# Taking the two column halves in turn: scan, banded heads, sparse heads and delta rule

## The chip, the cores and the metric

The kernel runs on one core of one Trainium2 chip, as one program. The metric is the device time of one execution in microseconds (us): the median over the runs shown. The trace is that of one further execution, taken with the hardware profiler. In what follows TensorE (rows of matmuls: PE, of weight loads: PEld) multiplies matrices into PSUM banks, VectorE (DVE), ScalarE (ACT) and GpSimd (POOL) work on tiles, and SyncE (SP) issues transfers.

## The reference, cut to what matters

Four layers on 512 tokens of width 1024, at batch 1. The first block is one layer with an SSD scan and differential attention, and one with retention and sliding-window attention; the second block has two layers, each with a gated delta rule, native sparse attention and stick-breaking attention, and a feed-forward part. Everything is float32. The changed products belong to these lines, head by head (all heads concerned are 64 wide; of the delta rule the kernel forms the products of `w` with the decayed keys and with the attention ahead of its recurrence):

```python
# scan: 16 heads in 4 groups, chunks of 128
y_diag = jnp.einsum("bclsg,bclsgr,bcsgrp->bclgrp", cb, decay_in, X)      # within a chunk
y_off = jnp.einsum("bclgn,bcgrpn,bclgr->bclgrp", Cc, state_prev, jnp.exp(a_cs))
# banded heads: 8 query heads, 2 key groups, window 128
out = jnp.einsum("bngrqk,bnkgd->bnqgrd", p, vb)
# delta rule: 6 heads, chunks of 64, state (64, 64)
v_new = u_i - jnp.einsum('bhcd,bhde->bhce', w_i, state)
# sparse heads: 6 query heads, 2 key groups, a selected and a window branch
o_s = jnp.einsum('bgrqn,bgqnd->bqgrd', p_s.astype(v_sel.dtype), v_sel)
o_w = jnp.einsum('bgrqn,bngd->bqgrd', p_w.astype(vw.dtype), vw)
```

## The kernel before

Activations lie feature-major: 128 features on the partitions, 512 tokens along the columns, one tile per 128 features. A projection (`fm`, lines 432 to 444) takes one unit of weights, splits it into a high and a low part (lines 409 and 411) and makes 24 products of 128x512 (`mm3`, lines 415 to 420: three for each of 8 chunks). These are the products of most of TensorE's time. Work of the heads stands between them.

Two heads of 64 features share one tile of 128 partitions. Where a product writes only one head, its stationary operand has 64 columns and its result goes to partitions 0 to 63 or 64 to 127 of a PSUM bank: to one half of the array's columns. Such a product of float32 operands is two instructions in the trace, each with its own weight load. A transpose is one. The four places that the change touches:

- **Scan** (`ssd`, line 848; products at 951 and 953). For each of 4 groups and 2 pairs of heads (`j`), a head `hh` makes `seg` (lines 938 to 943: one product into bank `s`, four VectorE subtractions, an exponential, a product with `cb`) and `ea` (lines 944 to 946), then for each of 4 chunks one product with `xdt` and, but for the first, one with the state `st`, all into its half of `py` (bank `o`). `seg` has two buffers, `ea` one.
- **Banded heads** (`swa`, line 1117; products at 1162). For each of 4 rounds `r` and 2 key groups `g`: the bias tile `stt` is loaded, then 4 query blocks go one after another through scores (lines 518, 519, bank `s`), VectorE's evacuation with the maximum (1150), ScalarE's exponential (1151), a scale (1155), one or two transposes (1158, bank `d`), a copy (1160) and the products. The tile `sl` has three buffers.
- **Delta rule** (`gdn_pair`, line 1331; products at 1469 and 1470). Of a pair of heads, head by head, 4 chunk pairs of two products each, into the banks `pA` and `pq` (bank `d`, two buffers). VectorE makes `aTz` of `pA` (1477), on which the recurrence over chunks rests.
- **Sparse heads** (`nsa_heads`, line 1639; products at 1671). For each of 3 heads `r`, 2 branches and 2 key groups: 4 query blocks with 1 to 4 key blocks each. The steps are those of the banded heads: scores, evacuation into `nl` (1660, 128 to 512 columns), exponential (1661), clamp, reciprocal and scale (1662 to 1664), transposes (1667, bank `t`, one buffer), copy into `npt` (1669), products into `po`, which accumulates over both branches. The `nl` tile's ring `nx` has three buffers.

Not changed, but of the same kind: the stick-breaking heads' products at line 1767 (loop from 1764) go over 4 key blocks and, inside, over the two heads, with 512, 384, 256 and 128 columns.

What sets the order: the program is written out once, and the tile framework arranges each engine's instructions ahead of time, by the place in the program and by when operands and buffers come free; products into one PSUM tile keep the program's order, and work on other tiles can be put between. On the chip each engine works its list in order. The list `ORDER` (line 305) says in which turn the delta rule (`g0` to `g2`), the inputs (`i`) and the sparse heads (`n0` to `n2`) are written, one stretch up to the next `yield` at a time. In `ssd` and `retention` the `fill` calls put an output projection's step between the heads' work.

Of the kernel before, what the change touches and what calls it, by code (L numbers as in the profile page):

```python
# [7 lines left out]
F32 = mybir.dt.float32  # L8
# [6 lines left out]
T = 512  # L15
# [326 lines left out]
class Build:  # L342
# [505 lines left out]
    def ssd(self, hs, p, outs, fill):  # L848
        nc = self.nc
# [29 lines left out]
        ps = self.bank("d")  # L879
# [8 lines left out]
        for g in range(4):  # L888
# [43 lines left out]
            nc.vector.tensor_mul(cb, ps, tri.rearrange("p (o l) -> p o l", o=1).to_broadcast([128, 4, 128]))  # L932
            for j in range(2):
                py = self.bank("o")
                for hh in range(2):
                    h = 4 * g + 2 * j + hh
                    pb = self.bank("s", [128, 4, 128])
                    nc.tensor.matmul(pb, sel[:, h:h + 1].to_broadcast([48, 128]), acsT, start=True, stop=True)
                    sg = p.tile([128, 4, 128], F32, tag="seg", name="seg", bufs=2)
                    for b in range(4):  # L940
                        nc.vector.tensor_scalar(sg[:, b], pb[:, b], acs[:, b, h:h + 1], 0.0, SUB, MIN)
                    nc.scalar.activation(sg, sg, ACTF.Exp)
                    nc.vector.tensor_mul(sg, sg, cb)
                    ea = p.tile([128, T], F32, tag="ea", name="ea")
                    nc.scalar.activation(ea, pb.rearrange("p b l -> p (b l)"), ACTF.Exp)
                    nc.vector.tensor_mul(ea, ea, ct)
                    c0 = 64 * (2 * j + hh)
                    for b in range(4):
                        s = slice(128 * b, 128 * b + 128)
                        o = py[64 * hh:64 * hh + 64, s]  # L950
                        nc.tensor.matmul(o, xdt[:, b, c0:c0 + 64], sg[:, b], start=True, stop=b == 0)
                        if b:
                            nc.tensor.matmul(o, st[:, b - 1, c0:c0 + 64], ea[:, s], start=False, stop=True)
                fill('ce'[j])
                y = outs.tile([128, T], F32, tag=f"s{2 * g + j}", name="ssdy")
                nc.vector.scalar_tensor_tensor(y, xts[j], self.V("eD")[:, 2 * g + j:2 * g + j + 1], py, MUL, ADD)
                for _, ps in self.fm("e_ssd", 6 * g + 4 + j, hs, side=True):
                    e = self.sigmoid(p, ps)
                    nc.vector.tensor_mul(e, e, ps)
                    nc.vector.tensor_mul(y, y, e)  # L960
                fill('df'[j])
                yield y
# [154 lines left out]
    def swa(self, hs, p, outs):  # L1117
# [15 lines left out]
        for r in range(4):  # L1133
            for _, ps in self.fm("o_sw", 2 + r, hs):
                qt = self.stack_left(p, "sqt", ps, 0.125, bufs=2)
            po = self.bank("o")
            for g in range(2):
                h = 4 * g + r
                gs = slice(64 * g, 64 * g + 64)
                tt = p.tile([128, 256], F32, tag="stt", name="stt", bufs=2)  # L1140
                nc.sync.dma_start(tt, self.t5[h][:, 256:512])
                nc.vector.tensor_add(tt, tt, self.C("wmask"))
                for i in range(4):
                    n = 256 if i else 128
                    k0 = 128 * (i - 1) if i else 0
                    s = self.bank("s")
                    self.scores(s[:, :256], qt, kt, g, slice(128 * i, 128 * i + 128), slice(k0, k0 + 256))
                    l = p.tile([128, 256], F32, tag="sl", name="sl", bufs=3)
                    sm = p.tile([128, 4], F32, tag="ssm", name="ssm", bufs=3)
                    nc.vector.tensor_tensor_reduce(l[:, :n], s[:, :n], tt[:, 256 - n:], -1.0, ns[:, h:h + 1], ADD, MIN, sm[:, 0:1])  # L1150
                    nc.scalar.activation(l[:, :n], l[:, :n], ACTF.Exp, bias=sm[:, 0:1], scale=-1.0, accum_out=sm[:, 1:2])
                    nc.scalar.activation(sm[:, 2:3], ns[:, h:h + 1], ACTF.Exp, bias=sm[:, 0:1], scale=-1.0)
                    nc.vector.tensor_add(sm[:, 3:4], sm[:, 1:2], sm[:, 2:3])
                    nc.vector.reciprocal(sm[:, 3:4], sm[:, 3:4])
                    nc.vector.tensor_scalar(l[:, :n], l[:, :n], sm[:, 3:4], None, MUL)
                    pt = self.bank("d", [128, 4, 128])
                    for j in range(n // 128):
                        nc.tensor.transpose(pt[:, j], l[:, 128 * j:128 * j + 128], ident)
                    ptt = p.tile([128, 2, 128], F32, tag="sptt", name="sptt", bufs=3)
                    nc.scalar.copy(ptt[:, :n // 128], pt[:, :n // 128])  # L1160
                    for j in range(n // 128):
                        nc.tensor.matmul(po[gs, 128 * i:128 * i + 128], vt[:, k0 // 128 + j, gs], ptt[:, j],
                                         start=j == 0, stop=j == n // 128 - 1)
            o = outs.tile([128, T], F32, tag="o", name="wo", bufs=5)
            nc.scalar.copy(o, po)
            yield o
# [164 lines left out]
    def gdn_pair(self, l, pr, hs, ab, p, outs, outs_):  # L1331
# [130 lines left out]
            nc.gpsimd.memset(qz[par][:, :, par2[1 - par]], 0.0)  # L1462

        pA, pq = pst(), pst()
        for hh in range(2):
            o = slice(64 * hh, 64 * hh + 64)
            for b in range(4):
                t = slice(128 * b, 128 * b + 128)
                mm(pA[o, t], wu[:, hh, b, 0:64], kdz[:, b, :, hh], start=True, stop=True)
                mm(pq[o, t], wu[:, hh, b, 0:64], attz[:, hh, b], start=True, stop=True)  # L1470


        aT = t8("nlt")
# [165 lines left out]
    def nsa_heads(self, l, r, st, p, on):  # L1639
# [7 lines left out]
        rr = slice(64 * (r % 2), 64 * (r % 2) + 64)  # L1647
        mm(po, st["vcb"][rr], st["ptc"][rr, r // 2], start=True, stop=False)
        for bi, br in enumerate("sw"):
            for g in range(2):  # L1650
                yield
                gs = slice(64 * g, 64 * g + 64)
                for i in range(4):
                    n = 128 * (i + 1)
                    s = self.bank("s")
                    w = max(n, 256)
                    self.scores(s[:, :w], ql, ks[br], g, slice(128 * i, 128 * i + 128), slice(0, w))
                    lt = p.tile([128, T], F32, tag="nx", name="nl", bufs=3)
                    sm = p.tile([128, 3], F32, tag="nsm", name="nsm", bufs=4)
# [2 lines left out]
                    nc.vector.tensor_scalar(sm[:, 1:2], sm[:, 1:2], 1e-30, None, MAX)  # L1662
                    nc.vector.reciprocal(sm[:, 2:3], sm[:, 1:2])
                    nc.vector.tensor_scalar(lt[:, :n], lt[:, :n], sm[:, 2:3], gates[:, i, 1 + bi, r, g:g + 1], MUL, MUL)
                    ps = self.bank("t", [128, 4, 128])
                    for j in range(i + 1):
                        nc.tensor.transpose(ps[:, j], lt[:, 128 * j:128 * j + 128], ident)  # L1667
                    pt = p.tile([128, 4, 128], F32, tag="npt", name="npt", bufs=2)
                    nc.scalar.copy(pt[:, 0:i + 1], ps[:, 0:i + 1])
                    for j in range(i + 1):  # L1670
                        mm(po[gs, 128 * i:128 * i + 128], vt[:, j, bi, gs], pt[:, j], start=False, stop=bi == 1 and i == 3 and j == 3)  # L1671
        yield
        o = qs
        nc.scalar.copy(o, po)
# [310 lines left out]
```

## Time and profile before

| | us |
|---|---|
| median of 3 runs | 3457.21 |
| lowest, highest run | 3454.8, 3462.34 |
| the profiled execution, its own time | 3465.89 |
| its span, first to last instruction | 3464.2 |
| TensorE matmul busy in the span | 3330.6 |
| VectorE busy | 2210.1 |
| ScalarE busy | 1693.8 |

Busy time is the union of an engine's instructions, so that overlapping ones count once. Matmuls are pipelined, and their ends are modelled: the duration of a matmul's row is longer than the step to the next matmul, and what a row of matmuls costs is read from their starts. A timeline row with xN merges N neighbours of one line: its length runs from the first one's start to the last one's end. Times in the timeline are us from the span's start.

### The profile page before, as it was taken

Reading aid. Unit: us, or ns where it says so; the run is one execution under the profiler, and the core shown is the slowest. Engines: PE = TensorE matmul, PEld = TensorE weight load, DVE = VectorE, ACT = ScalarE, POOL = GpSimd, SP = SyncE. Lnnn points to the kernel's source line nnn. Section 1 sums busy time; section 2 is a strip of 40 time slices with the busy share of each in tenths; the row PEclk is TensorE's granted clock in tenths of the full one; section 3 lists DMA queues with packets and bytes.
Section 4 is the critical chain, followed back from the end, with each engine's and each line's share of the span. In section 5 each row is a group of like instructions: output and inputs, shape, how many; then the busy total and the mean of one; then the engine's idle time right before and its main releaser. Section 6 shows DMA issues by size and latency. Waiting matters only on the chain. (4 is left out here: it accounts for less than half of the span.)

```text
span 3464.2 us, 45651 instructions
## 1 busy us (share of the span) xinstructions
PE 3330.6 (96%) x17752; PEld 2620.7 (76%) x17752; DVE 2210.1 (64%) x3650; ACT 1693.8 (49%) x2962; POOL 298.2 (9%) x204
## 2 busy tenths in 40 slices
PE   8999998999989998999899999999989999999997
PEld 4877775888868876888667777888877777788885
DVE  6678775544476655444566765776776676677676
ACT  4665554322365445222355557544455565654444
POOL 2000111000110002000201001000030100200002
PEclk9999998999999999999999999999999999999998
DMA  7343212532333442322221002232322100233322
GB/s 261 117 144 105 72 61 68 171 121 92 100 107 105 157 135 99 97 91 98 79 77 62 19 28 84 93 97 98 98 88 74 62 19 22 79 98 98 98 91 76
DMA packets 97112, 323.93 MB, mean 94 GB/s; under 512 B 10936, under 2 KB 12472, under 8 KB 96768
## 3 DMA queue, kind: packets, MB, share of 16 engines
q1 hardware_dynamic: 96160, 319.44, 28.5%
q8 instruction: 140, 2.29, 0.3%
q10 hardware_dynamic: 576, 1.05, 0.1%
q14 instruction: 76, 0.62, 0.1%
q0 software_dynamic: 160, 0.52, 0.0%
HBM read 313.61 MB, written 9.98 MB: 93 GB/s over the span
## 5 line engine op out<-in xcount | busy, mean ns | idle before, releaser
L409 ACT CAST whi<-wr 128x1024 fp32r<-128x1024 f32 x459 | 480.3, 1048 | 884.9 <-PE pss L419 421.8
L411 DVE TENSOR_TENSOR wlo<-wr,whi 128x1024 fp32r<-128x1024 f32 x409 | 501.9, 1228 | 388.8 <-ACT whi L409 384.6
L418 PE MATMUL psg<-hh,whi 128*128 128x512 f32 x1448 | 582.9, 403 | 8.1 <-DVE gu L837 7.4
L420 PE MATMUL psg<-hh,wlo 128*128 128x512 f32 x1448 | 577.7, 399 | 0.0
L419 PE MATMUL psg<-hl,whi 128*128 128x512 f32 x1448 | 576.7, 398 | 0.0
L418 PE MATMUL pss<-hh,whi 128*128 128x512 f32 x784 | 310.7, 399 | 31.1 <-ACT hh L475 11.3
L418 PEld LDWEIGHTS psg<-hh,whi 128*128 128x128 f32 x1448 | 274.3, 189 | 69.2 <-issue 8.8
L420 PEld LDWEIGHTS psg<-hh,wlo 128*128 128x128 f32 x1448 | 273.4, 189 | 58.8 <-issue 6.7
L419 PEld LDWEIGHTS psg<-hl,whi 128*128 128x128 f32 x1448 | 273.7, 189 | 57.4 <-issue 7.3
L419 PE MATMUL pss<-hl,whi 128*128 128x512 f32 x784 | 312.3, 398 | 3.3 <-DVE hl L482 3.3
L420 PE MATMUL pss<-hh,wlo 128*128 128x512 f32 x784 | 311.0, 397 | 0.0
L334 POOL TENSOR_TENSOR sqacc<-sqacc,sq 128x512 f32<-128x512 f32 x86 | 130.3, 1515 | 1703.4 <-ACT sq L332 1702.5
L418 PE MATMUL psg<-mh,whi 128*128 128x512 f32 x560 | 223.7, 400 | 1.1 <-DVE x L680 1.0
L420 PE MATMUL psg<-mh,wlo 128*128 128x512 f32 x560 | 220.7, 395 | 0.0
L419 PE MATMUL psg<-ml,whi 128*128 128x512 f32 x560 | 220.2, 394 | 0.0
L418 PEld LDWEIGHTS pss<-hh,whi 128*128 128x128 f32 x784 | 150.2, 192 | 70.2 <-ACT hh L475 16.0
L419 PEld LDWEIGHTS pss<-hl,whi 128*128 128x128 f32 x784 | 151.1, 193 | 38.5 <-DVE hl L482 4.9
L411 POOL TENSOR_TENSOR wlo<-wr,whi 128x1024 fp32r<-128x1024 f32 x50 | 122.8, 2456 | 631.4 <-ACT whi L409 631.4
L420 PEld LDWEIGHTS pss<-hh,wlo 128*128 128x128 f32 x784 | 150.7, 192 | 33.8 <-issue 2.0
L418 PE MATMUL pss<-mh,whi 128*128 128x512 f32 x432 | 170.9, 396 | 0.5 <-DVE x L680 0.5
L420 PE MATMUL pss<-mh,wlo 128*128 128x512 f32 x432 | 169.8, 393 | 0.0
L419 PE MATMUL pss<-ml,whi 128*128 128x512 f32 x432 | 169.7, 393 | 0.0
(628 smaller groups left out, 6399.7 us busy)
## 6 DMA issues: line engine op xcount, KB each, us to landing
wr<-w SPq DMA_DIRECT2D x128, 512.0 KB, 3.5
wr<-up SPq DMA_DIRECT2D x88, 512.0 KB, 3.4
mw<-modw SPq DMA_DIRECT2D x80, 512.0 KB, 3.8
wr<-in SPq DMA_DIRECT2D x48, 512.0 KB, 3.5
wr<-down SPq DMA_DIRECT2D x40, 512.0 KB, 3.5
wr<-e_ssd SPq DMA_DIRECT2D x24, 512.0 KB, 3.5
wr<-e_qk SPq DMA_DIRECT2D x16, 512.0 KB, 4.1
mw<-modw SPq DMA_DIRECT2D x32, 256.0 KB, 5.4
```

Of the source, the lines that this page charges most:

```text
L334: nc.gpsimd.tensor_add(self.acc, self.acc, sq)
L409: self.nc.scalar.copy(hi, raw)
L411: eng.tensor_sub(lo, raw, hi.bitcast(F32))
L418: mm(ps, ws[0], xs[0], start=first, stop=False)
L419: mm(ps, ws[0], xs[1], start=False, stop=False)
L420: mm(ps, ws[1], xs[0], start=False, stop=last)
```

## The change

In all four places two products that write different halves now follow each other. In the scan both heads' `seg` and `ea` are made first, then each chunk's products are issued for head 0 and head 1; the second head's `ea` takes a slot of the shared ring `pt` (three buffers). In the banded heads the loop over key groups moves inside the loop over query blocks; both bias tiles are loaded first (`stt` has four buffers instead of two), the transposes of both groups go to one bank, and one copy (`sptt`, two buffers of twice the size instead of three) serves both. In the delta rule the loops over chunk pairs and heads change places. In the sparse heads the loop over key groups moves inside too; transposes, copies and products go by up to two key blocks of both groups at a time, and the `yield`s move from before each group to before query blocks 0 and 3.

```diff
@@ -932,6 +932,7 @@
             nc.vector.tensor_mul(cb, ps, tri.rearrange("p (o l) -> p o l", o=1).to_broadcast([128, 4, 128]))
             for j in range(2):
                 py = self.bank("o")
+                sgs, eas = [], []
                 for hh in range(2):
                     h = 4 * g + 2 * j + hh
                     pb = self.bank("s", [128, 4, 128])
@@ -941,16 +942,21 @@
                         nc.vector.tensor_scalar(sg[:, b], pb[:, b], acs[:, b, h:h + 1], 0.0, SUB, MIN)
                     nc.scalar.activation(sg, sg, ACTF.Exp)
                     nc.vector.tensor_mul(sg, sg, cb)
-                    ea = p.tile([128, T], F32, tag="ea", name="ea")
+                    ea = self.nb.tile([128, T], F32, tag="pt", name="ea", bufs=3) if hh else p.tile([128, T], F32, tag="ea", name="ea")
                     nc.scalar.activation(ea, pb.rearrange("p b l -> p (b l)"), ACTF.Exp)
                     nc.vector.tensor_mul(ea, ea, ct)
-                    c0 = 64 * (2 * j + hh)
-                    for b in range(4):
-                        s = slice(128 * b, 128 * b + 128)
-                        o = py[64 * hh:64 * hh + 64, s]
-                        nc.tensor.matmul(o, xdt[:, b, c0:c0 + 64], sg[:, b], start=True, stop=b == 0)
-                        if b:
-                            nc.tensor.matmul(o, st[:, b - 1, c0:c0 + 64], ea[:, s], start=False, stop=True)
+                    sgs.append(sg)
+                    eas.append(ea)
+
+                for b in range(4):
+                    s = slice(128 * b, 128 * b + 128)
+                    for hh in range(2):
+                        c0 = 64 * (2 * j + hh)
+                        nc.tensor.matmul(py[64 * hh:64 * hh + 64, s], xdt[:, b, c0:c0 + 64], sgs[hh][:, b], start=True, stop=b == 0)
+                    if b:
+                        for hh in range(2):
+                            c0 = 64 * (2 * j + hh)
+                            nc.tensor.matmul(py[64 * hh:64 * hh + 64, s], st[:, b - 1, c0:c0 + 64], eas[hh][:, s], start=False, stop=True)
                 fill('ce'[j])
                 y = outs.tile([128, T], F32, tag=f"s{2 * g + j}", name="ssdy")
                 nc.vector.scalar_tensor_tensor(y, xts[j], self.V("eD")[:, 2 * g + j:2 * g + j + 1], py, MUL, ADD)
@@ -1134,15 +1140,18 @@
             for _, ps in self.fm("o_sw", 2 + r, hs):
                 qt = self.stack_left(p, "sqt", ps, 0.125, bufs=2)
             po = self.bank("o")
+            tts = []
             for g in range(2):
-                h = 4 * g + r
-                gs = slice(64 * g, 64 * g + 64)
-                tt = p.tile([128, 256], F32, tag="stt", name="stt", bufs=2)
-                nc.sync.dma_start(tt, self.t5[h][:, 256:512])
+                tt = p.tile([128, 256], F32, tag="stt", name="stt", bufs=4)
+                nc.sync.dma_start(tt, self.t5[4 * g + r][:, 256:512])
                 nc.vector.tensor_add(tt, tt, self.C("wmask"))
-                for i in range(4):
-                    n = 256 if i else 128
-                    k0 = 128 * (i - 1) if i else 0
+                tts.append(tt)
+            for i in range(4):
+                n = 256 if i else 128
+                k0 = 128 * (i - 1) if i else 0
+                pt = self.bank("d", [128, 2, 2, 128])
+                for g in range(2):
+                    h, tt = 4 * g + r, tts[g]
                     s = self.bank("s")
                     self.scores(s[:, :256], qt, kt, g, slice(128 * i, 128 * i + 128), slice(k0, k0 + 256))
                     l = p.tile([128, 256], F32, tag="sl", name="sl", bufs=3)
@@ -1153,13 +1162,15 @@
                     nc.vector.tensor_add(sm[:, 3:4], sm[:, 1:2], sm[:, 2:3])
                     nc.vector.reciprocal(sm[:, 3:4], sm[:, 3:4])
                     nc.vector.tensor_scalar(l[:, :n], l[:, :n], sm[:, 3:4], None, MUL)
-                    pt = self.bank("d", [128, 4, 128])
                     for j in range(n // 128):
-                        nc.tensor.transpose(pt[:, j], l[:, 128 * j:128 * j + 128], ident)
-                    ptt = p.tile([128, 2, 128], F32, tag="sptt", name="sptt", bufs=3)
-                    nc.scalar.copy(ptt[:, :n // 128], pt[:, :n // 128])
-                    for j in range(n // 128):
-                        nc.tensor.matmul(po[gs, 128 * i:128 * i + 128], vt[:, k0 // 128 + j, gs], ptt[:, j],
+                        nc.tensor.transpose(pt[:, j, g], l[:, 128 * j:128 * j + 128], ident)
+                ptt = p.tile([128, 2, 2, 128], F32, tag="sptt", name="sptt", bufs=2)
+                nc.scalar.copy(ptt[:, :n // 128], pt[:, :n // 128])
+
+                for j in range(n // 128):
+                    for g in range(2):
+                        gs = slice(64 * g, 64 * g + 64)
+                        nc.tensor.matmul(po[gs, 128 * i:128 * i + 128], vt[:, k0 // 128 + j, gs], ptt[:, j, g],
                                          start=j == 0, stop=j == n // 128 - 1)
             o = outs.tile([128, T], F32, tag="o", name="wo", bufs=5)
             nc.scalar.copy(o, po)
@@ -1462,12 +1473,12 @@
             nc.gpsimd.memset(qz[par][:, :, par2[1 - par]], 0.0)
 
         pA, pq = pst(), pst()
-        for hh in range(2):
-            o = slice(64 * hh, 64 * hh + 64)
-            for b in range(4):
-                t = slice(128 * b, 128 * b + 128)
-                mm(pA[o, t], wu[:, hh, b, 0:64], kdz[:, b, :, hh], start=True, stop=True)
-                mm(pq[o, t], wu[:, hh, b, 0:64], attz[:, hh, b], start=True, stop=True)
+        for b in range(4):
+            t = slice(128 * b, 128 * b + 128)
+            for hh in range(2):
+                mm(pA[64 * hh:64 * hh + 64, t], wu[:, hh, b, 0:64], kdz[:, b, :, hh], start=True, stop=True)
+            for hh in range(2):
+                mm(pq[64 * hh:64 * hh + 64, t], wu[:, hh, b, 0:64], attz[:, hh, b], start=True, stop=True)
 
 
         aT = t8("nlt")
@@ -1647,13 +1658,14 @@
         rr = slice(64 * (r % 2), 64 * (r % 2) + 64)
         mm(po, st["vcb"][rr], st["ptc"][rr, r // 2], start=True, stop=False)
         for bi, br in enumerate("sw"):
-            for g in range(2):
-                yield
-                gs = slice(64 * g, 64 * g + 64)
-                for i in range(4):
-                    n = 128 * (i + 1)
+            for i in range(4):
+                if i in (0, 3):
+                    yield
+                n = 128 * (i + 1)
+                w = max(n, 256)
+                ls = []
+                for g in range(2):
                     s = self.bank("s")
-                    w = max(n, 256)
                     self.scores(s[:, :w], ql, ks[br], g, slice(128 * i, 128 * i + 128), slice(0, w))
                     lt = p.tile([128, T], F32, tag="nx", name="nl", bufs=3)
                     sm = p.tile([128, 3], F32, tag="nsm", name="nsm", bufs=4)
@@ -1662,13 +1674,21 @@
                     nc.vector.tensor_scalar(sm[:, 1:2], sm[:, 1:2], 1e-30, None, MAX)
                     nc.vector.reciprocal(sm[:, 2:3], sm[:, 1:2])
                     nc.vector.tensor_scalar(lt[:, :n], lt[:, :n], sm[:, 2:3], gates[:, i, 1 + bi, r, g:g + 1], MUL, MUL)
-                    ps = self.bank("t", [128, 4, 128])
-                    for j in range(i + 1):
-                        nc.tensor.transpose(ps[:, j], lt[:, 128 * j:128 * j + 128], ident)
-                    pt = p.tile([128, 4, 128], F32, tag="npt", name="npt", bufs=2)
-                    nc.scalar.copy(pt[:, 0:i + 1], ps[:, 0:i + 1])
-                    for j in range(i + 1):
-                        mm(po[gs, 128 * i:128 * i + 128], vt[:, j, bi, gs], pt[:, j], start=False, stop=bi == 1 and i == 3 and j == 3)
+                    ls.append(lt)
+                for j0 in range(0, i + 1, 2):
+                    nj = min(2, i + 1 - j0)
+                    ps = self.bank("t", [128, 2, 2, 128])
+                    for j in range(nj):
+                        for g in range(2):
+                            nc.tensor.transpose(ps[:, j, g], ls[g][:, 128 * (j0 + j):128 * (j0 + j) + 128], ident)
+                    pt = p.tile([128, 2, 2, 128], F32, tag="npt", name="npt", bufs=2)
+                    nc.scalar.copy(pt[:, 0:nj], ps[:, 0:nj])
+
+                    for j in range(nj):
+                        for g in range(2):
+                            gs = slice(64 * g, 64 * g + 64)
+                            mm(po[gs, 128 * i:128 * i + 128], vt[:, j0 + j, bi, gs], pt[:, j, g],
+                               start=False, stop=bi == 1 and i == 3 and j0 + j == 3)
         yield
         o = qs
         nc.scalar.copy(o, po)
```

## Rows read from the trace of the kernel before

**Rows 1.** The page's first part: busy us of each engine, share of span, instructions.

```profile
PE 3330.6 (96%) x17752; PEld 2620.7 (76%) x17752; DVE 2210.1 (64%) x3650; ACT 1693.8 (49%) x2962; POOL 298.2 (9%) x204
```

**Rows 2.** Busy us by stretch: PE, PEld, DVE, ACT, POOL; PEclk, DMA, GB/s.

```profile
319.00:512.00 193.00, 192.74 (x934) 147.89 (x933) 135.10 (x227) 107.18 (x167) 26.59 (x12) 1.00 0.23 74
1012.00:1070.00 58.00, 57.87 (x365) 43.98 (x365) 41.61 (x171) 40.38 (x138) 0.00 (x0) 1.00 0.25 78
...
1897.00:2005.00 108.00, 106.23 (x935) 78.97 (x935) 79.16 (x221) 68.60 (x166) 8.66 (x6) 1.00 0.06 21
2760.00:2930.00 170.00, 167.27 (x1627) 126.75 (x1626) 114.70 (x333) 94.74 (x238) 12.98 (x10) 1.00 0.07 21
```

**Rows 3.** Matmuls by source line: count, ns min/median/max, first and last start, forms.

```profile
L951 PE MATMUL pso<-seg,xdt x128: 272/273/323, 319.0 to 511.6; 128*64 128x128 f32 x128
...
L953 PE MATMUL pso<-ea,sst x96: 272/273/323, 320.0 to 511.9; 128*64 128x128 f32 x96
...
L1162 PE MATMUL pso<-sptt,svt x112: 272/273/323, 1012.9 to 1069.5; 128*64 128x128 f32 x112
...
L1469 PE MATMUL psd<-kdz,wu x96: 272/273/323, 1813.1 to 2913.0; 128*64 128x128 f32 x96
...
L1671 PE MATMUL pso<-npt,nvt x480: 272/273/324, 1901.8 to 2928.8; 128*64 128x128 f32 x160
```

**Rows 4.** PE timeline, delta rule: start, length, engine, line, tiles, form, count.

```profile
1813.12 1.09 PE L1469 MATMUL psd<-kdz,wu 128*64 128x128 f32 x8
...
1814.59 0.27 PE L1470 MATMUL psd<-attz,wu 128*64 128x128 f32 x1
1814.64 0.27 PE L1469 MATMUL psd<-kdz,wu 128*64 128x128 f32 x1
1814.69 0.44 PE L1470 MATMUL psd<-attz,wu 128*64 128x128 f32 x4
...
1816.06 0.38 PE L1470 MATMUL psd<-attz,wu 128*64 128x128 f32 x2
```

**Rows 5.** PE timeline, first heads of the scan.

```profile
319.01 0.65 PE L951 MATMUL pso<-seg,xdt 128*64 128x128 f32 x4
319.59 0.50 PE L420 MATMUL psg<-hi,wlo 128*128 128x512 f32 x1
320.02 0.43 PE L953 MATMUL pso<-ea,sst 128*64 128x128 f32 x2
...
321.65 0.40 PE L419 MATMUL psg<-lo,whi 128*128 128x512 f32 x1
321.88 0.39 PE L420 MATMUL psg<-hi,wlo 128*128 128x512 f32 x1
```

**Rows 6.** PE timeline, the products of the stick-breaking heads.

```profile
2112.86 2.34 PE L1767 MATMUL pso<-at,sbv 128*64 128x512 f32 x14
```

**Rows 7.** The copies by source line, columns as in rows 3.

```profile
L1669 ACT COPY npt<-pst x96: 254/437/603, 1898.9 to 2927.3; 128x128 f32<-128x128 f32 x24, 128x256 f32<-128x256 f32 x24, 128x384 f32<-128x384 f32 x24, 128x512 f32<-128x512 f32 x24
...
L1160 ACT COPY sptt<-psd x32: 249/372/377, 1012.6 to 1068.7; 128x256 f32<-128x256 f32 x24, 128x128 f32<-128x128 f32 x8
```

**Rows 8.** The chain of a sparse head's key group by source line.

```profile
L1660 DVE CUSTOM_DVE_ANT_0 nl<-pss,sconst x96: 263/483/693, 1889.6 to 2917.6; 128x128 f32<-128x128 f32 x24, 128x256 f32<-128x256 f32 x24, 128x384 f32<-128x384 f32 x24, 128x512 f32<-128x512 f32 x24
L1660 DVE DVE_READ_ACCUMULATOR2_ANT nsm<- x96: 76/84/90, 1889.8 to 2918.3; 128x1 f32 x96
...
L1661 ACT ACTIVATE nl<-nl,nsm x96: 387/560/728, 1892.1 to 2918.4; 128x128 f32<-128x128 f32 x24, 128x256 f32<-128x256 f32 x24, 128x384 f32<-128x384 f32 x24, 128x512 f32<-128x512 f32 x24
L1661 ACT ACTIVATION_READ_ACCUMULATOR nl<-nl,nsm x96: 185/190/218, 1892.4 to 2919.0; 128x1 f32 x96
...
L1664 DVE TENSOR_SCALAR nl<-nl,nsm,abtok x96: 335/442/1507, 1895.9 to 2920.1; 128x128 f32<-128x128 f32 x24, 128x256 f32<-128x256 f32 x24, 128x384 f32<-128x384 f32 x24, 128x512 f32<-128x512 f32 x24
```

**Rows 9.** Waits: engine line, waited for; us in total, times, longest us.

```profile
DVE aTz L1477 <- PE psd L1469: 27.2, 6, 5.4
...
DVE nl L1660 <- PE pst L1667: 24.6, 30, 2.1
```

## The prediction

> **What bounds the kernel now.** I read the page first, for the engine that is full: TensorE is busy 96% of the span, VectorE 64% [rows 1]. That is a mean over unlike stages, so the next view is the table by stretch, for the four stages in which the changed lines run: the scan (319 to 512 us), the banded heads (1012 to 1070) and the two layers of sparse heads and delta rule (1897 to 2005, 2760 to 2930) [rows 2]. In each of them TensorE is busy 98 to 100% of the stretch, at a granted clock of 1.00, the 2.4 GHz level, while VectorE has 70, 72, 73 and 67%. TensorE sets the pace there, and what its products cost is read from their starts. A product onto half of the columns is two instructions (128 of line 951 for 64 products) [rows 3]. Their durations of 0.27 us overlap; the cost is the step from one start to the next. The run of eight at 1813.12 is 1.09 us long, its last instruction 0.27, its first step 0.16 (below): six steps are left in 0.66 us, **0.11 us each** [rows 4].
>
> **The change, part by part.**
>
> *Halves in turn.* The rows that decide are those around 1814.6 [rows 4]: line 1470 of one head and line 1469 of the other, which write different halves, start at 1814.59, 1814.64, 1814.69, 0.05 us apart, and each still lasts 0.27. Two halves together thus keep each its 0.11, and a pair costs one step instead of two. The products of line 1767, where the program already takes the halves in turn, say the same: 14 instructions in 2.34 us [rows 6]. They hold 2 x 512 + 4 x (384 + 256 + 128) = 4096 columns, which at 0.11 us for 128 would be 3.5 us one after another; the longer half alone has 2560 columns, 2.2 us. So I take half a step saved, 0.055 us, for each changed instruction. The rule against it is in the Trainium skill, "TensorE: Matmul & The Clock Gate", the section on packing small matmuls: a weight load overlaps a running matmul only when the row groups differ. All these products use all 128 rows, so by that rule this term would be zero; rows 4 and 6 disagree with it.
>
> Counts [rows 3]: sparse heads 480 instructions, 26 us; banded heads 112, 6.1 us; scan 128 + 96 = 224, 12.3 us. For the delta rule lines 1469 and 1470 have 96 each, but part of them already overlaps: a run begins at 1813.12 and its last start is at 1816.06 + 0.11, so 3.05 us [rows 4]; in turn it would be 0.16 + 14 x 0.11 = 1.7. Six runs save 8.2 us.
>
> *Fewer changes of shape.* Each run of half-column products between full-width ones pays at both ends [rows 5]. The last of the run at 319.01 starts at 319.39 and the next full product at 319.59, 0.20 instead of 0.11. From that to the next run at 320.02 is 0.43, where line 419 to 420 takes 0.23 undisturbed; and the first two of that run are 0.16 apart. Over the usual steps: 0.09 + 0.20 + 0.05 = 0.34 us for a run. Next to transposes it is less; I take 0.3. Sparse heads: one copy, one run, so 96 runs [rows 7]; by the diff, six copies for a pair of key groups over its four query blocks instead of eight, so 72: 7.2 us. Banded: 32 copies become 16, 4.8 us. Scan: I counted 27 runs in the timeline between 319.0 and 511.9; the eight blocks of the new loop make 8 if nothing breaks them. But the products of one PSUM tile stay in program order, so the first head's now stand behind the second head's seg and ea, and TensorE will put other work between: I take 19 runs, 2.4 us, with ends 0 and 5.7. Delta rule: 6 stay 6.
>
> *Sum on TensorE:* sparse 33.2, banded 10.9, scan 14.7, delta rule 8.2: **67 us**.
>
> *What is added.* Both groups' nl tiles are now live at once, of three nx buffers. The next pair's first group can go ahead; its second must wait for the last transposes. VectorE already waits for those, 24.6 us in 30 times [rows 9]. Behind a waiting evacuation stand all later VectorE instructions, the weight remainders of line 411 among them, for which the projections wait. The price is bounded by zero (other PE work covers it, as the projections and the delta rule do now) and by the whole chain from scores to transposes, uncovered: 0.48 + 0.08 + 0.56 + 0.19 + 0.44 = 1.75 us [rows 8] for each of 2 x 3 x 2 x 4 = 48 pairs, 84 us. I take a quarter of the gain in the sparse heads, 8 us, nearer to zero, since the full TensorE of rows 2 shows that there is covering work. In the banded heads, likewise with two of three sl buffers, 10.9 of 58 us go from TensorE, and 47 us have to hold 41.6 us of VectorE work [rows 2]: I take 65%. In the scan both seg buffers stay taken until a block's end; VectorE has 135 us of 193, so 90%. In the delta rule VectorE waits for line 1469, 27.2 us in six times [rows 9], so its gain passes whole.
>
> *Moved at no cost.* The second stt load of a banded round (8 loads, unchanged) is issued ahead of the first group's work on SP's queue, into four buffers instead of two; that round's first evacuation wants only the first. The second head's ea goes into a pt slot, beside the squares of the norms; without that cover one ScalarE exponential waits for one norm. Copies become fewer: from 254 ns for 128 columns to 603 for 512 the fixed part is about 0.14 us [rows 7], 24 times 0.14 off ScalarE, which is not the bound. The new places of the yields only shift which filler comes when.
>
> *What reaches the end:* 25 + 7.1 + 13.2 + 8.2 = **53 us**. The profiled execution took 3465.9 us (span 3464.2), 8.7 above the median; 53 off it is 3413, and off the median of 3457.2, **3404**.
>
> **The rivals.**
>
> *A, a new wait takes half.* The pairs run into the nl wait, VectorE becomes the bound in the banded heads and the sparse ones (193.9 of 278 us now, of 245 after) [rows 2]. For it: the waits of rows 9. Against: the full TensorE. With 0.55 us uncovered for each of 48 pairs, 26 us more are lost: 3430.
>
> *B, the turns do nothing.* Either the weight loads of the other half don't run beside a product (this is the rule named above), or filler falls between the two halves. Left are the fewer changes of shape: 7.2 + 4.8 + 2.4 = 14 us, so 3443. Against it stand rows 4 and 6, and that a PSUM tile's products keep their order.
>
> *C, slower.* The pair's wait is wholly uncovered: in the sparse heads, at the nl evacuation of line 1660, the next pair's second group starts its chain only after this pair's last transposes, and TensorE, in order, stands. 84 us against 33 there and 28 gained elsewhere: 3457 + 23 = 3480. It decides from (33 + 28) / 48 = 1.3 us uncovered for a pair. For it: 24.6 us of such waits with one group at a time. Against: delta rule and projections interleave with every head.
>
> **How the numbers follow.** Forecast 0.60; A 0.21; B 0.08; C 0.07; more than forecast, 0.04: with 8 runs in the scan (3.3 us more) and nothing lost, 70 to 72 us go, so 3385, the low end. The high end leaves out B, C and the worst of A: 20 us gained, 3437. The forecast's own range is 3387 to 3417. A measurement of this kernel tells about 0.2%, 7 us, from no change. Faster by more than that: the forecast, more than it, nearly all of A and most of B, 0.90. Slower: C but for its mild end, 0.06. Within: 0.04.
>
> **What would show it.** Right: the products of these lines start in pairs, some hundredths of a us apart, a pair every 0.11; the busy time of line 1671 drops by a third or more; the 108 and 170 us of the sparse stretches shrink by some 12 each, the scan's 193 by 13; waits of line 1660 for line 1667 grow less than the gain. Wrong: single steps of 0.11 through a whole run (B), or TensorE idle ahead of the transposes and the copies of the pairs (A, C), or half-column runs cut into pairs by fillers.

## The result and the profile after

The median of 4 runs is **3419.75 us** (3409.84 to 3426.16) against 3459.78 for the kernel before on the same chip (4 runs, 3454.8 to 3469.43): 40 us less, ratio **0.9878** [0.9844, 0.9913]. Forecast were 53 us less, 3404 with a range of 3385 to 3437. The result lies in the range, nearer to its upper end; it is 3 us above the forecast's own range of 3387 to 3417, between the forecast and rival A (3430). The profiled execution took 3426.16 (span 3424.4), 6 above the median. Lines after the first hunk move: 951 and 953 are now 955 and 959, 1162 is 1173, 1469 and 1470 are 1479 and 1481, 1660 is 1672, 1667 is 1683, 1671 is 1690.

The page's first part, kernel after (beside [rows 1]):

```profile
PE 3280.0 (96%) x17752; PEld 2580.1 (75%) x17752; DVE 2216.6 (65%) x3650; ACT 1690.6 (49%) x2922; POOL 294.3 (9%) x204
```

Busy time by source line and form: busy us, mean ns of one, then the idle time before. Kernel before:

```profile
L1671 PE MATMUL pso<-npt,nvt 128*64 128x128 f32 x480 | 74.7, 284 | 1.1 <-ACT npt L1669 1.0
L1162 PE MATMUL pso<-sptt,svt 128*64 128x128 f32 x112 | 18.7, 286 | 0.1
```

Kernel after:

```profile
L1690 PE MATMUL pso<-npt,nvt 128*64 128x128 f32 x480 | 46.8, 293 | 1.4 <-ACT npt L1685 1.4
L955 PE MATMUL pso<-seg,xdt 128*64 128x128 f32 x128 | 16.7, 284 | 1.1 <-DVE seg L944 1.1
L1173 PE MATMUL pso<-sptt,svt 128*64 128x128 f32 x112 | 9.6, 287 | 0.0
```

The count and the duration of one are as in [rows 3]; the union shrank by 37% in the sparse heads and by half in the banded ones, so instructions that followed each other now lie side by side. The timeline of the delta rule shows how (kernel after, TensorE; the same work as [rows 4]):

```profile
1792.85 0.43 PE L1479 MATMUL psd<-kdz,wu 128*64 128x128 f32 x2
...
1794.10 0.32 PE L1479 MATMUL psd<-kdz,wu 128*64 128x128 f32 x1
1794.11 0.32 PE L1481 MATMUL psd<-attz,wu 128*64 128x128 f32 x1
1794.26 0.27 PE L1479 MATMUL psd<-kdz,wu 128*64 128x128 f32 x1
1794.27 0.38 PE L1481 MATMUL psd<-attz,wu 128*64 128x128 f32 x2
...
1795.58 0.48 PE L1481 MATMUL psd<-attz,wu 128*64 128x128 f32 x3
1795.99 0.50 PE L420 MATMUL psg<-hh,wlo 128*128 128x512 f32 x1
```

Two instructions of different halves start 0.01 us apart, a pair every 0.11. Thirty instructions go from 1794.10 to the next full product at 1795.99, 1.9 us; before, 32 went from 1813.12 to a last start at 1816.06 + 0.11 [rows 4]. A run of eight in the sparse heads was 1.09 us long before:

```profile
1922.55 1.09 PE L1671 MATMUL pso<-npt,nvt 128*64 128x128 f32 x8
```

and is 0.66 in the kernel after:

```profile
1958.18 0.66 PE L1690 MATMUL pso<-npt,nvt 128*64 128x128 f32 x8
```

Summed over the starts, from the first product of a run to the next other instruction, the runs of the sparse heads and the delta rule took 90.7 us before and 54.6 after, those of the banded heads 16.6 and 8.5, those of the scan 28.0 and 17.1: 55 us less on TensorE (the first step into a run isn't counted).

Not all of it reached the end. The stretches, kernel after (scan, banded heads, the two layers of sparse heads; columns as in [rows 2]):

```profile
316.00:499.00 183.00, 181.93 (x943) 140.09 (x943) 139.42 (x230) 106.92 (x168) 22.78 (x12) 1.00 0.24 78
1001.00:1047.50 46.50, 46.48 (x359) 37.95 (x359) 39.91 (x158) 36.92 (x116) 0.00 (x0) 1.00 0.27 86
1867.00:2047.00 180.00, 171.48 (x1697) 127.22 (x1697) 129.56 (x363) 108.66 (x254) 14.96 (x11) 0.98 0.08 26
2717.00:2913.00 196.00, 187.45 (x1813) 142.52 (x1813) 140.48 (x380) 123.18 (x278) 14.93 (x11) 0.98 0.09 27
```

The work of the third row stood here before, in a stretch from its first score to the end of its last head:

```profile
1889.00:2075.00 186.00, 183.28 (x1695) 138.22 (x1695) 127.98 (x367) 110.13 (x269) 15.38 (x11) 1.00 0.08 25
```

In scan and banded heads TensorE stays full and the stretch shrinks by about what the runs give (10 and 11.5 us). In the sparse heads TensorE's busy time falls by 11.8 us and the stretch only by 6: the idle time of TensorE rises from 2.7 to 8.5 us, and the granted clock is no longer 1.00. The largest hole (timeline of the kernel after, TensorE and VectorE):

```profile
1989.88 0.60 PE L1427 MATMUL psd<-const,gv 128*128 128x128 f32 x4
1990.21 1.38 DVE L1424 TENSOR_TENSOR kdz<-psd,kds 64x512 f32<-64x512 f32 x2
1991.63 0.69 DVE L1428 TENSOR_TENSOR R<-psd,abtok 128x512 f32<-128x512 f32 x1
1992.23 0.72 DVE L1436 COPY_PREDICATED dT<-levels,nlt 128x512 f32<-128x512 uint8 x1
...
1993.10 0.63 PE L1445 MATMUL psd<-const,dT 128*128 128x128 f32 x4 [2.62 <-DVE nsm L1674]
```

TensorE stands for 2.6 us behind a queue of VectorE work. In this hole no evacuation waits for a transpose: VectorE is busy 6.8 of the 7 us from 1987 to 1994, and such a wait last ended at 1924.9. Of all 8.5 idle us of TensorE in the stretch, VectorE is busy in 8.4. Right behind the hole the clock is at its lower level, 1.2 GHz, for 6.8 us:

```profile
1994.40:2001.20 6.80, 6.75 (x80) 5.12 (x81) 3.35 (x7) 2.14 (x6) 0.00 (x0) 0.50 0.36 110
```

At 0.50 this costs some 3.4 us more. The second layer shows the same pair, hole and 6.8 us at half clock; before, neither layer had a half-clock stretch there.

As milestones I took the starts of the 10,440 projection products (lines 418 to 420), which both traces have in the same order; the gap between the two traces at one of them is what was gained until then. By these, the scan gave 12.4 us (2.4 more stood ahead of its first changed product), the banded heads 9.8, and each of the two layers of delta rule and sparse heads 8.1. Some 3 us went again in the retention, where VectorE waits 2.5 us for a load. No edit is shown to be behind that: of the kernels below, `three_parts` and `banded_alone` lose nothing there, and `sparse_nl_two_rings`, whose banded heads are as before, loses 3.6.

### The profile page after: what moved, and what is told of

Read it like the earlier page. It is cut to its first block, busy times and chain, and to the rows that moved or that the text cites. A ratio compares the mean times of both kernels' runs of the same rounds, so it can differ in the third digit from the quotient of the medians.

```text
span 3424.4 us, 45576 instructions
## 1 busy us (share of the span) xinstructions
PE 3280.0 (96%) x17752; PEld 2580.1 (75%) x17752; DVE 2216.6 (65%) x3650; ACT 1690.6 (49%) x2922; POOL 294.3 (9%) x204
## 3 DMA queue, kind: packets, MB, share of 16 engines
q1 hardware_dynamic: 96160, 319.44, 28.5%
```

## The experiments

Two theories stood for the part that is missing in the sparse heads. One: VectorE's work now comes in bursts, and the projections that covered it are used up. The other, "nx": a pair of key groups holds two of three `nx` buffers, so that the next evacuation waits for transposes, with all of VectorE's queue behind it. All ratios are to the kernel before, on the same chip.

**Parts alone.** Each kernel has only some of the diff's hunks, here by their headers: the first two are the scan's, the next two the banded heads', then the delta rule's, the last two the sparse heads'. `three_parts` leaves out the last two.

```diff
@@ -932,6 +932,7 @@
@@ -941,16 +942,21 @@
...
@@ -1134,15 +1140,18 @@
@@ -1153,13 +1162,15 @@
...
@@ -1462,12 +1473,12 @@
...
@@ -1647,13 +1658,14 @@
@@ -1662,13 +1674,21 @@
```

> Scan, banded heads and delta rule as changed, the sparse heads as before. By landmarks (the same projection products in both traces) the changed kernel is 14.9 us ahead after the scan, and 9.7 more after the banded heads, of which 3 go again in the retention. Theory 1 (the sparse change itself gave back about half of its 33 us, the rest came as forecast): 14.9 + 6.5 + 8.2 for the delta rule = 30 us off the kernel before, ratio 0.9915. Rival (the delta rule's turns gave nothing at the end, the sparse heads gave all of what the two layers gained): 21 us off, ratio 0.994.

> Only the sparse heads as changed. Theory 1 (TensorE runs out of cover while VectorE works off its bursts): 10 to 14 us off, ratio 0.996 to 0.997, with idle steps of TensorE ahead of the delta rule's transposes as in the full change. If the loss came from the delta rule's faster products meeting the sparse ones, the part alone gains more: 20 us and over, ratio 0.994 or less.

> The change in the scan alone. By the forecast 13.2 us reach the end: 0.9962. By the starts of the projections in the full change 15 us: 0.9957. If VectorE, which has 135 of 193 us there, or the pt ring took it back: 0.998 or more.

> The change in the banded heads alone. By the forecast 7.1 us reach the end: 0.9980. If the 9.7 us that the full change gained over that stage stay: 0.9972. If all that was gained is given back behind it, in the retention and its work on VectorE: 1.000.

> The change in the delta rule alone: turns and nothing else, no joined runs, no new buffers. The forecast's 8.2 us pass whole if the overlap of the halves is worth 0.055 us an instruction and VectorE waits for line 1469: 0.9976. By the stretches of the run with three parts, where each layer lost 2.8 us there, 5.6 us: 0.9984. If products of two halves do not overlap in turn (rival B): 1.000.

| kernel | median us | ratio | us less by the ratio |
|---|---|---|---|
| three_parts | 3432.58 | 0.9916 [0.9901, 0.993] | 29 |
| sparse_alone | 3466.78 | 1.0005 [0.9995, 1.0015] | -2 |
| scan_alone | 3448.39 | 0.9959 [0.9941, 0.9977] | 14 |
| banded_alone | 3452.99 | 0.9967 [0.9955, 0.9979] | 11 |
| delta_alone | 3451.98 | 0.9965 [0.9953, 0.9978] | 12 |

Three parts gave 29 us where the forecast's terms for them add up to 28.5. Run singly, the three add up to 37 by the ratios, which the intervals allow. By the milestones the scan alone gave 12.4, the banded heads alone 9.6 and nothing of that went back, the delta rule 4.3 and 4.4 in the two layers, 31 together; `delta_alone`'s trace has 8 us more where no changed product runs, by the clock (last section), and its median of 12 may hold some of that. The sparse part alone gave nothing, less than was expected of it. Its stretch, beside that of before above:

```profile
1886.00:2073.00 187.00, 175.83 (x1695) 130.63 (x1696) 128.93 (x367) 109.97 (x257) 15.27 (x11) 0.96 0.08 25
```

TensorE is busy 7.5 us less and stands 8.5 us longer. The mean granted clock is 0.96, which costs some 7 us of the busy time.

**The buffers.** The second group's tile goes to another ring, in the full change (`nl_in_pt`), in the sparse part alone (`sparse_nl_two_rings`), and, as a control, for every second query block in the kernel before (`before_nl_two_rings`, with `if i % 2`):

```diff
-                    lt = p.tile([128, T], F32, tag="nx", name="nl", bufs=3)
+                    lt = self.nb.tile([128, T], F32, tag="pt", name="nl", bufs=3) if g else p.tile([128, T], F32, tag="nx", name="nl", bufs=3)
```

> The full change, with the second key group's nl in the shared ring pt, so that the first group's alone have the three nx buffers. Theory 1 (bursts on VectorE): within 4 us of the full change, about 3417 to 3424. Rival (the pair holds two of three nx buffers, and the next pair's evacuation waits): the waits of the nl evacuation for the transposes fall away and 8 us or more come back, 3412 or less.

> The change in the sparse heads alone, with the second key group's nl tile in the shared ring pt instead of nx. Theory 'nx': a pair holds two of three nx buffers, and the next pair's evacuation waits for transposes; without that wait the sparse heads give what was forecast for them, 25 us: ratio 0.992 to 0.994, and no wait of the nl evacuation for the transposes is left. Rival 'bursts': what TensorE then waits for is VectorE's work that comes in bursts and filler that was used up, and the buffers have little to do with it: 0.998 to 1.001, as with the sparse part alone (1.0005).

> The kernel before, with every second query block's nl tile in the ring pt. Theory 'nx': its 24.6 us of such waits on VectorE lie beside a full TensorE, so taking them away gives nothing: 0.9985 to 1.001. Rival 'more buffers help whatever the order': the 12 to 15 us that the same step gave on top of the full change come here too: 0.9955 to 0.9965.

Measured: `nl_in_pt` **3404.83, 0.9835** [0.9819, 0.9852], 57 us less and 15 below the full change; `sparse_nl_two_rings` 3444.24, 0.994 [0.9927, 0.9954], 21 us less where the same part without the second ring gave none; `before_nl_two_rings` 3462.56, 0.9993 [0.9979, 1.0007], nothing, though its waits for the transposes fall from 24.6 to 7.0 us. So the buffer is worth much with the change and nothing without it. By the milestones the two layers gain 14.7 and 14.3 us in `nl_in_pt` for 8.1 each in the full change, and 11.3 each in the sparse part with the second ring for -0.9 and 0.2 without: 13 and 23 us for the buffer. What line 1672 waited for, kernel after (the view by source line: us in total, times):

```profile
  PE pst L1683: 16.2, 12
  PE pss L519: 2.2, 6
```

and in `nl_in_pt`:

```profile
  PE pss L519: 6.0, 17
```

The waits for the transposes are gone. Their length does not give their price: in sum they were shorter than before (24.6 us [rows 9]), fewer and longer (1.35 us each for 0.82), and in the kernel after, as in that before, TensorE is busy through every one of them. TensorE stands elsewhere, while VectorE works. That VectorE, held up in these waits, comes late with what TensorE needs next would fit, but is not shown. The stretches of `nl_in_pt`:

```profile
1855.00:2028.00 173.00, 168.38 (x1694) 125.30 (x1693) 125.64 (x367) 108.13 (x258) 14.56 (x11) 1.00 0.09 27
2694.00:2883.00 189.00, 183.20 (x1798) 138.20 (x1797) 137.91 (x387) 120.07 (x280) 15.29 (x12) 1.00 0.09 29
```

Each is 7 us shorter than after the full change: 3.9 of the first are idle time of TensorE, 3.1 its busy time, about what the lower clock cost; the clock is 1.00 again. What the runs don't separate: the framework arranges the program by when buffers come free, so that with another ring the order of the filler changes too. Wait and order were taken away together.

**Less VectorE work.** The full change without the clamp ahead of the reciprocal (`no_clamp`), and this with the two rings (`full_two_rings_no_clamp`); the sum that the clamp bounds from below is used as it is.

```diff
-                    nc.vector.tensor_scalar(sm[:, 1:2], sm[:, 1:2], 1e-30, None, MAX)
```

> The full change without the clamp of the row sums in the sparse heads (96 small VectorE instructions of 0.148 us, 14.2 us in all; the sums stay above the bound in these heads, so the output is the same). Theory 1 (VectorE sets the pace in the bursts): 4 to 9 us less than the full change. Rival (buffers or ScalarE copies set it): within 2 us.

> The full change with the second group's nl tile in the ring pt, and without the clamp ahead of the reciprocal (96 VectorE instructions of 0.06 to 0.15 us; the sum it bounds is left unbounded). Theory 'nx': with the waits for nx gone the sparse stage is short of nothing that the clamps hold up, so little is added to the two rings' 0.9835: 0.982 to 0.984. Rival 'VectorE': the clamps were worth 6 us on top of the full change (0.9859 against 0.9878) and are worth as much here: 0.981 to 0.982.

Measured: `no_clamp` 3417.13, 0.9859 [0.9838, 0.988], 49 us less, 7 below the full change. That is where the first theory put it (4 to 9), but the intervals don't tell it from nothing. The trace says more. Its stretch in the first layer:

```profile
1868.00:2042.00 174.00, 168.89 (x1692) 124.23 (x1691) 121.57 (x314) 107.76 (x253) 14.47 (x11) 0.99 0.08 27
```

and its waits for the transposes (us in total, times, longest):

```profile
DVE nl L1672 <- PE pst L1682: 6.3, 12, 1.0
```

The stretch is 6 us shorter than after the full change and 1 us longer than in `nl_in_pt`; by the milestones the layers gain 13.3 and 13.0 us instead of 8.1 each, and the waits for the transposes fall from 16.2 to 6.3 us with the ring as it was. So less work on VectorE does in the traces most of what the second ring does, and the two theories are not told apart here: the first is not out. With both edits, 3409.59, 0.9847 [0.9827, 0.9866], the median is not told from that of `nl_in_pt`; the layers gain 16.6 each, 4 us more than there in all. `nl_in_pt` has the lowest median of all kernels run.

**Order inside a run.** `no_turns` keeps the joined runs, copies and buffers, but issues one half's products first and then the other's (in the sparse heads; scan and banded heads alike, the delta rule as before):

```diff
-                    for j in range(nj):
-                        for g in range(2):
-                            gs = slice(64 * g, 64 * g + 64)
+                    for g in range(2):
+                        gs = slice(64 * g, 64 * g + 64)
+                        for j in range(nj):
```

> The full change, but inside every run the products of one half of the columns come first and those of the other half after them (scan, banded heads, sparse heads; the delta rule as before). The joined runs, copies and buffers of the change stay. If the turns are what saves (0.055 us for each of 1008 instructions, 55 us on TensorE), a run of eight is about 1.09 us long again instead of 0.66, and only the fewer changes of shape are left, 14 us on TensorE with some 8 at the end: ratio to before 0.996 to 0.999. If the joining and the new order of the work made the gain and the turns little, it stays near the full change: 0.988 to 0.990.

Measured: 3451.39, 0.9963 [0.9949, 0.9978], 13 us less. The ratio came as expected and the reason did not. A run of eight in `no_turns`:

```profile
1901.02 0.66 PE L1688 MATMUL pso<-npt,nvt 128*64 128x128 f32 x8 [0.67 <-ACT npt L1683]
```

It is as short as in turn. The program has four instructions of one half and then four of the other, and they start in pairs all the same. In the median of such runs of eight the starts span 0.392 us here and 0.385 after the full change, against 0.815 before. The banded heads gained 9.7 us by the milestones, as in turn. What `no_turns` lost it lost in the scan (2 us gained instead of 12.4) and in the two layers (-1 us instead of 16), where the delta rule is as before; in scan and delta rule one head's instructions are 10 to 16 in a row. (The sparse part alone, in turn, had given nothing in the layers either.) In the scan all products of a pair of heads go into one PSUM bank, so that the program's order is kept; a run of 24 in `no_turns`, ten of the first head and then fourteen of the second:

```profile
320.92 0.43 PE L957 MATMUL pso<-ea,sst 128*64 128x128 f32 x2
...
321.41 0.38 PE L957 MATMUL pso<-ea,sst 128*64 128x128 f32 x2
321.63 0.44 PE L955 MATMUL pso<-seg,xdt 128*64 128x128 f32 x4
...
322.99 0.38 PE L957 MATMUL pso<-ea,sst 128*64 128x128 f32 x2
```

The second head's first instruction starts at 321.63 beside the seventh of the first head's ten, 0.005 us after it, while three of the first head are still to start; before and behind these the steps are 0.11. How far TensorE reaches, `reach` shows: the kernel before with blocks of 4, 8 and 16 instructions of one half in the first, second and third pair of the delta rule.

```diff
+        nb = (1, 2, 4)[pr]
+        for b0 in range(0, 4, nb):
+            for hh in range(2):
+                for b in range(b0, b0 + nb):
...
```

> The kernel before, with other block lengths in the delta rule's run: in the first pair of heads the halves change after every 4 instructions, in the second after every 8, in the third after 16 (as before). Theory 'reach': TensorE starts a product of the other half while up to about four earlier ones of the first half still wait, so that order inside a run counts only beyond that. With steps of 0.11 us and a reach of four, from the first start to the last: 1.7 to 1.8 us for blocks of 4, 2.1 to 2.2 us for 8 (the second half begins four steps late, then all overlaps), 2.9 us for 16. Rival 'neighbours': only products that stand next to each other overlap, so that a border saves one step: about 2.6, 3.1 and 2.9 to 3.3 us.

Blocks of 4, `reach`, TensorE's timeline (the run is broken by three full products behind its first two):

```profile
1806.23 0.32 PE L1471 MATMUL psd<-attz,wu 128*64 128x128 f32 x1
1806.24 0.32 PE L1470 MATMUL psd<-kdz,wu 128*64 128x128 f32 x1
1806.39 0.27 PE L1471 MATMUL psd<-attz,wu 128*64 128x128 f32 x1
...
1807.82 0.38 PE L1471 MATMUL psd<-attz,wu 128*64 128x128 f32 x2
1808.13 0.50 PE L420 MATMUL psg<-hh,wlo 128*128 128x512 f32 x1
```

Blocks of 16:

```profile
2039.81 1.09 PE L1470 MATMUL psd<-kdz,wu 128*64 128x128 f32 x8
2040.74 0.71 PE L1471 MATMUL psd<-attz,wu 128*64 128x128 f32 x5
2041.18 0.32 PE L1470 MATMUL psd<-kdz,wu 128*64 128x128 f32 x1
2041.28 0.27 PE L1471 MATMUL psd<-attz,wu 128*64 128x128 f32 x1
...
2042.76 0.38 PE L1471 MATMUL psd<-attz,wu 128*64 128x128 f32 x2
```

With 4, thirty instructions take 1.90 us to the next full product, the same as in turn. With 16, twelve starts 0.11 apart come first (2039.81 to 2041.06), then the second half's first product at 2041.18 beside the thirteenth of the first half; the last start is at 2042.87, 3.06 us after the first. With 8, the run is broken behind its first four instructions, and the last 28 take 1.82 us from the first start to the last. "Reach" said 1.7 to 1.8, 2.1 to 2.2 and 2.9; "neighbours" 2.6 for blocks of 4, and it falls by these. The broken run of 8 tests neither, and for 16 both come near. The median of one run, 3455.28, says little.

## Why the prediction was right, and where it was not

- **Half a step for an instruction** about held in size: 55 us by the starts, some 7 of which are the fewer ends of runs (167 runs became 120, 0.09 at the end and 0.05 at the first step of each), leaves 48, where 1008 instructions of 0.055 make 55. Its reason was too narrow. Products of two halves overlap when they are in one run and the second half's first is not more than about four instructions behind. So in sparse and banded heads it is the joined run that saves, and the turns add next to nothing (0.385 us for 0.392); in scan and delta rule, with 10 to 16 instructions of one half in a row, the turns are needed. I had ascribed all of it to the turns and to the joining only the changes of shape; that the size came out in sparse and banded heads is luck so far, since the change brought the joined runs along.
- **Fewer changes of shape**: 16 runs in the banded heads as forecast, 20 in the scan (forecast 19), 78 in the sparse heads, four of them joined with the delta rule's (forecast 72). The delta rule's six did not stay six: four are broken behind their first two instructions. On TensorE 67 us were forecast, against the 55 by the starts, without the step into a run.
- **Rival B** is out. The Trainium skill, "TensorE: Matmul & The Clock Gate", the section on packing small matmuls, lets a weight load overlap a running matmul only when the row groups differ, and has matmuls start in program order. These use the same 128 rows, each with its own weights, and start 0.01 us apart; in `no_turns` the fifth of a run starts ahead of the second. Here the measurement decides.
- **What passes through**, scan 13.2, banded 7.1, delta rule 8.2: 28.5 forecast, 29 measured for the three. By the milestones 12.4, 9.8 and 8.7; the banded heads lost less than I took off, with VectorE busy 40 of 46.5 us and TensorE still full.
- **The failed step is the price of the sparse heads' pairs, which I put on the held nx buffers.** I took 8 of 33 us, "nearer to zero, since the full TensorE of rows 2 shows that there is covering work". By the ratios the full change kept 42 - 29 = 13 us there instead of 25 (by the milestones 7), and the part alone none; with a second ring it kept 21 alone and 57 - 29 = 28 in the full change (by the milestones 23 and 20). The buffer, with the order that follows from it, thus cost 13 to 23 us. Rows 2 show TensorE full at the old pace, and their first sparse stretch ends with 80 of the layer's 240 instructions of line 1671 still to come. The change takes some 12 us a layer from TensorE and nothing from VectorE (128.0 us in the first layer before, 129.6 after), and TensorE then stands while VectorE works. The rise in idle time (5.8 us a layer) is thus rival A's second half, VectorE as the bound, in the sparse heads alone; that TensorE stands in the nx wait itself, as A and C had it, the trace does not show. To it came the lower clock behind the largest hole, which no case had. By which way the held buffers make VectorE late stays open, since the clamps' removal does much the same.
- Of the signs named, the pairs, the drop of line 1671's busy time and the scan came; the sparse stretches shrank by 6 and some 7 us instead of 12, part of which is the delta rule's. That line 1660's waits would grow by less than the gain was no good sign: in sum they shrank, and the forecast was still missed. A sign of rival A came as well, TensorE idle ahead of the pairs' transposes, 2.2 us in the first layer against 1.0 before.

## What to carry over

Work for different column halves overlaps when it stands within a few instructions of one another: bring it into one run first, and alternate only where one half's run is longer than about four. When products that are computed in pairs double the live tiles of a ring, give the ring the second set; a buffer that is worth nothing under a full TensorE can be worth much when the change takes work from TensorE and leaves VectorE its own. A control in the kernel before (the buffer alone: nothing) tells such an interaction from a plain gain.

## What was not expected of the hardware

TensorE starts matmuls of another half ahead of earlier ones of the first: in blocks of 16 the second half's first start comes with three instructions of the first half still to start, in `no_turns` 0.014 us after the run's first. That each engine works its list in order, as was said ahead of the prediction, does not hold for these starts.

The granted clock makes much of the spread. The four runs after the change took spans of 3408.1, 3414.6, 3421.5 and 3424.4 us at mean clocks of 0.986, 0.984, 0.983 and 0.982. One stretch at the lower clock lies ahead of the delta rule's first changed product, in work that no edit touches (kernel after):

```profile
1738.40:1755.50 17.10, 17.10 (x67) 11.36 (x67) 7.58 (x14) 4.22 (x10) 0.00 (x0) 0.50 0.09 32
```

It stands in the profiled runs of before and of seven other kernels, the kernel after among them, and is missing, in whole or in part, in those of `nl_in_pt`, `no_turns`, `sparse_alone`, `delta_alone`, `reach` and `full_two_rings_no_clamp`; there the projections behind it come up to 8 us sooner. What decides it stays open, so differences of that size between two single traces are not read as an effect of an edit.
